# Sums of squares from two rounded parts instead of one float32 product, in a GLA and MLA layer

## The chip, the core and the metric

The kernel runs on one core of one Trainium2 chip. The metric is the device time of one execution in microseconds (us); lower is better. Three runs of the kernel before gave 1149.85, 1149.23 and 1146.63 us, so the median is 1149.23 us.

## What is computed

The reference is two layers over 1024 latent tokens of width 1024. The first layer mixes tokens by gated linear attention (GLA, 4 heads, value width 128) and by multi-head latent attention (MLA); the second by Fourier mixing and spatial gating. Only two places of the first layer matter here, both an RMS normalisation:

```python
def rms_norm(x, g):
    xf = x.astype(jnp.float32)
    y = xf * lax.rsqrt(jnp.mean(xf * xf, -1, keepdims=True) + LN_EPS)
    return (y * g.astype(jnp.float32)).astype(x.dtype)
...
    y_gla = rms_norm(o_gl, gla_norm_g).reshape(B, n, GLA_V_W).astype(h_lat.dtype) * jax.nn.silu(gg_l)
...
    kv = jnp.einsum('bnr,re->bne', rms_norm(ckv, kv_norm_g), w_ukv)...
...
    q = jnp.einsum('bnr,re->bne', rms_norm(cq, q_norm_g), w_uq)...
```

The GLA outputs are normalised per head over 128 channels. The query latents `cq` (rank 256) and the key and value latents `ckv` (rank 128) are normalised over their rank.

## The kernel before, in words

Activations lie transposed, with channels on the 128 partitions and tokens along the free dimension. A sum over channels is therefore a TensorE product with a 128x128 matrix of ones, `k.ones`, which also leaves the sum on every partition.

Most products of the kernel are not plain float32. A tensor is split by `split` (L131) into a rounded part `hi` of type float32r, cast on ScalarE (L136), and a rest `lo`, subtracted on VectorE (L141), and `mm3` (L144) multiplies such parts in three float32r products (L146 to L148). The sums of squares are an exception: they are plain float32 products.

**The GLA outputs** are made by `gla_b` (L673), once for each of four heads, in two halves of 512 tokens. A half is summed in a PSUM bank `po` (L733, L736), squared by ScalarE into `sq` (L741), and after a yield multiplied by the ones (L744). Logarithm and exponential on ScalarE turn the sum into the inverse root, VectorE scales `po` by it (L749), and a transfer that POOL issues puts the result into DRAM (L750). That is 8 sums of 512 columns.

**The latents** are normalised by `rms_T` (L814). It loads one or two blocks (L820), squares them (L824), sums the squares with the ones (L828), refines the inverse root on VectorE (L836 to L839), scales (L843) and stores (L844). `rms_ckv` (L847) calls it for blocks of 512, 512 and 256 tokens with one part; `rms_cq` (L852) for two blocks of 512 with two parts. That is 7 float32 products, 6 of 512 columns and one of 256.

**Order.** The work is written as generators that yield a cost, and `weave` (L51) always advances the stream that is furthest behind its budget. `rms_ckv` runs between the first two heads' `gla_a`, woven with the projection of the GLA values (L486) and with `ada_rest` (L771), which adds up modulation weights on VectorE (L805). `rms_cq` runs beside `gla_b` of the third head. All of `gla` is woven with `in_proj_b` (L531), which projects the input by three-product groups and evacuates each group through a scratch tile `ev` (L189 to L191). The tile framework then fixes the order of each engine's instructions when the program is built, and that is not strictly the order of the source.

**Buffers.** Scratch tiles of 128x512 come from `w2` (L97), a pool of 8 buffers that all streams share. PSUM banks come from a pool of 8. ScalarE table loads for another function are held behind all earlier uses of the old table (`act`, L108).

Of the kernel before, what the change touches and what calls it, by code (L numbers as in the profile page):

```python
# [12 lines left out]
F32 = mybir.dt.float32  # L13
F32R = mybir.dt.float32r
# [6 lines left out]
P = 128  # L21
# [10 lines left out]
def f32(ap):  # L32
    return ap.bitcast(F32)
# [184 lines left out]
def consts(k):  # L218
    nc, A = k.nc, k.A
    c = k.cpool  # L220
    k.ident = c.tile([P, P], F32, name="ident")
    make_identity(nc, k.ident)
    k.eps_c = c.tile([P, 1], F32, name="eps_c")
    nc.vector.memset(k.eps_c, EPS)
    k.one_c = c.tile([P, 2], F32, name="one_c")
    nc.vector.memset(k.one_c, 1.0)
    k.mhalf = c.tile([P, 32], F32, name="mhalf")
    nc.vector.memset(k.mhalf, -0.5)
    k.ones = c.tile([P, P], F32, name="ones")
    nc.vector.memset(k.ones, 1.0)  # L230


def load_norm(k, src):
# [436 lines left out]
    yield 4.0  # L670


def gla_b(k, hd, S):  # L673

    nc = k.nc
    T = nc.tensor
# [23 lines left out]
    for i in range(15):  # L700
        nc.vector.scalar_tensor_tensor(
            out=Tst[(i + 1) // 8][:, (i + 1) % 8, :], in0=Tst[i // 8][:, i % 8, :], scalar=w[:, i:i + 1],
# [9 lines left out]
    for b in range(2):  # L712
# [6 lines left out]
        for c in range(2):  # L719
            r = slice(64 * c, 64 * c + 64)  # L720
            v = [x[r].rearrange("p (t x) -> p t x", x=P)[:, :, r] for x in pa]
# [6 lines left out]
    for b in range(2):  # L728
        att = k.att[:, b]
        po = k.bank("pso")  # L730
        for t in range(4):
            i = 4 * b + t
            T.matmul(po[:, t * P:(t + 1) * P], k.gv[i // 2][:, i % 2, vs], att[:, t, :], start=True, stop=False)  # L733
            for c in range(2):
                ch = 2 * i + c
                T.matmul(po[:, t * P + 64 * c:t * P + 64 * c + 64], Tch[ch // 8][:, ch % 8, :], qh[:, ch * 64:ch * 64 + 64], start=False, stop=c == 1)  # L736
            if t == 1:
                yield 1.3

        sq = k.w2(name="sq")  # L740
        nc.scalar.activation(out=sq, in_=po, func=AF.Square)  # L741
        yield 2.0
        pv = k.bank("psvar")
        T.matmul(pv, k.ones, sq, start=True, stop=True)  # L744
        rs = sq
        k.act(rs, pv, AF.Ln, scale=1.0 / P, bias=k.eps_c)
        k.act(rs, rs, AF.Exp, scale=-0.5)
        og = k.w2(name="og")
        nc.vector.scalar_tensor_tensor(out=og, in0=po, scalar=k.gng, in1=rs, op0=ALU.mult, op1=ALU.mult)  # L749
        nc.gpsimd.dma_start(k.ogd[hd][:, b * 512:(b + 1) * 512], og)  # L750
        yield 2.0
# [5 lines left out]
def gla(k):  # L757
    k.ogd = [k.spill(f"ogd{i}") for i in range(4)]
    k.att = k.b4(F32, (P, 2, 4, P), name="att")
    k.nc.gpsimd.memset(k.att, 0.0)  # L760
    for hd in range(4):
        st = [(gla_b(k, hd, k.S[hd]), 24.0)]
        if hd < 2:
            st.append((gla_a(k, hd + 2, k.S[hd + 2]), 20.0))
        elif hd == 2:
            st.append((rms_cq(k), 12.0))
        yield from weave(*st)
    k.gla_done = True
# [45 lines left out]
def rms_T(k, dr, o, rank):  # L814

    nc = k.nc
    n = o.stop - o.start
    x = [k.w2(name="rmx") for _ in dr]
    for i, d in enumerate(dr):
        nc.sync.dma_start(x[i][:, :n], d[:, o])  # L820
    yield 1.0
    sq = [k.w2(name="rms") for _ in range(2)]
    for i in range(len(dr)):
        nc.scalar.activation(out=sq[i][:, :n], in_=x[i][:, :n], func=AF.Square)  # L824
    yield 1.0
    v = k.bank("psrms")
    for i in range(len(dr)):
        nc.tensor.matmul(v[:, :n], k.ones, sq[i][:, :n], start=i == 0, stop=i == len(dr) - 1)  # L828
    yield 1.0
    y, q = sq[0][:, :n], sq[1][:, :n]  # L830
    t = k.w2(name="rmt")
    k.act(y, v[:, :n], AF.Ln, scale=1.0 / rank, bias=k.eps_c)
    k.act(y, y, AF.Exp, scale=-0.5)

    nc.scalar.activation(out=q, in_=y, func=AF.Square)
    nc.vector.tensor_scalar(out=t[:, :n], in0=v[:, :n], scalar1=1.0 / rank, scalar2=EPS, op0=ALU.mult, op1=ALU.add)  # L836
    nc.vector.tensor_tensor(out=t[:, :n], in0=t[:, :n], in1=q, op=ALU.mult)
    nc.vector.tensor_scalar(out=t[:, :n], in0=t[:, :n], scalar1=-0.5, scalar2=1.5, op0=ALU.mult, op1=ALU.add)
    nc.vector.tensor_tensor(out=y, in0=t[:, :n], in1=y, op=ALU.mult)  # L839
    for i, d in enumerate(dr):  # L840
        xi = x[i][:, :n]
        g = k.mlag[:, i:i + 1] if len(dr) == 2 else k.mlag[:, 2:3]
        nc.vector.scalar_tensor_tensor(out=xi, in0=xi, scalar=g, in1=y, op0=ALU.mult, op1=ALU.mult)  # L843
        nc.gpsimd.dma_start(d[:, o], xi)  # L844


def rms_ckv(k):  # L847
    for s, n in KBLK:
        yield from rms_T(k, [k.ckvd], slice(s, s + n), 128)


def rms_cq(k):  # L852
    assert k.cq_done
    for s in range(0, N, 512):
        yield from rms_T(k, k.cqd, slice(s, s + 512), 256)
        yield 3.0
# [752 lines left out]
```

## Time and profile before

| | us |
|---|---|
| median of 3 runs | 1149.23 |
| the profiled execution | 1150.0 |
| its span, first to last instruction | 1147.5 |
| TensorE matmul (PE) busy in the span | 1091.7 |
| VectorE (DVE) busy | 739.0 |
| ScalarE (ACT) busy | 556.6 |
| GpSimd (POOL) busy | 260.1 |

PE is the matmul side of TensorE and PEld its weight loads, which overlap the matmuls. The mean granted TensorE clock of the span was 0.985 of full speed. Rows of a timeline give the start, the duration and the instruction, with the idle time before it in brackets; the end of a matmul is modelled, so the start of the next one says how long TensorE was taken.

### The profile page before, as it was taken

How to read it: one execution, taken by the hardware profiler on the slowest of the kernel's cores; microseconds unless marked ns; L12 is line 12 of the kernel's file. 1: busy time of each engine (PE TensorE's matmuls, PEld its weight loads, DVE VectorE, ACT ScalarE, POOL GpSimd, SP SyncE). 2: the span in 40 equal slices, each digit the busy share in tenths (PEclk: the TensorE clock that was granted, in tenths of full speed). 3: DMA queues.
4: the chain of work that ended last, by engine and by line, in shares of the span. 5: the costliest groups of instructions: out<-in, count | busy, mean ns of one | idle time of the engine just before them, and what ended most of it. 6: DMA issues, size and time to landing. Idle time of an engine off the chain costs nothing.

```text
span 1147.5 us, 14546 instructions
## 1 busy us (share of the span) xinstructions
PE 1091.7 (95%) x5288; PEld 864.4 (75%) x5288; DVE 739.0 (64%) x1256; ACT 556.6 (49%) x956; POOL 260.1 (23%) x260
## 2 busy tenths in 40 slices
PE   5889999899999999999999999999999999999997
PEld 3668778677777777767677666888788888888885
DVE  6867784756655675765778677788526533664544
ACT  6285755576553367857767778313422223332000
POOL 3520000000000023332424466343101000022111
PEclk8989999899999999999999999999999999999999
DMA  9635662333435752113202424323400311125111
GB/s 373 243 127 194 210 229 101 118 119 111 183 120 178 240 156 52 24 47 88 66 4 51 124 74 137 121 110 134 160 1 1 109 38 56 55 69 200 62 55 55
DMA packets 41752, 131.89 MB, mean 115 GB/s; under 512 B 5673, under 2 KB 7465, under 8 KB 41682
## 3 DMA queue, kind: packets, MB, share of 16 engines
q1 hardware_dynamic: 35578, 114.77, 30.5%
q0 software_dynamic: 3312, 10.26, 2.3%
q10 hardware_dynamic: 2792, 5.94, 1.3%
q8 instruction: 41, 0.67, 0.2%
q14 instruction: 29, 0.24, 0.1%
HBM read 98.37 MB, written 20.36 MB: 103 GB/s over the span
## 4 chain that ended last, share of the span: by engine, by line
PE 75%; DVE 8%; ACT 7%; issue 4%; POOL 3%; DMA 3%; SPq 1%; POOLq 0%; DVEq 0%; ACTq 0%
PE ps L146 10%; PE ps L147 10%; PE ps L148 10%; PE pso L146 5%; PE pso L147 5%; PE pso L148 5%; PE pss L1068 3%; PE psm L993 3%; PE pss L1069 3%; PE pss L1070 3%; PE psav L1054 3%; PE psav L1053 2%; PE psav L1052 2%; PE psn L146 1%; PE psn L147 1%
## 5 line engine op out<-in xcount | busy, mean ns | idle before, releaser
L141 POOL TENSOR_TENSOR ph<-pexp,ph 128x512 fp32r<-128x512 f32 x80 | 108.2, 1357 | 167.8 <-ACT ph L136 145.3
L118 ACT ACTIVATE pexp<-pss 128x512 f32<-128x512 f32 x160 | 93.2, 596 | 61.1 <-PE pss L1070 59.4
L146 PE MATMUL ps<-h,hi 128*128 128x512 f32 x256 | 103.8, 417 | 7.4 <-ACT h L328 3.3
L994 DVE TENSOR_REDUCE mx<-psm 128x1 f32<-128x512 f32 (+1 forms) x192 | 102.5, 592 | 10.7 <-PE psm L993 10.3
L148 PE MATMUL ps<-h,lo 128*128 128x512 f32 x256 | 102.6, 401 | 2.8 <-DVE lo L305 1.5
L147 PE MATMUL ps<-h,hi 128*128 128x512 f32 x256 | 104.2, 407 | 0.8 <-DVE h L329 0.8
L141 DVE TENSOR_TENSOR ph<-pexp,ph 128x512 fp32r<-128x512 f32 x80 | 75.1, 943 | 44.6 <-ACT ph L136 42.9
L141 DVE TENSOR_TENSOR lo<-wraw,hi 128x1024 fp32r<-128x1024 f32 x37 | 47.1, 1283 | 85.0 <-ACT hi L136 80.0
L146 PE MATMUL pso<-hi,yh 128*128 128x512 f32 x256 | 99.8, 390 | 0.0
L147 PE MATMUL pso<-lo,yh 128*128 128x512 f32 x256 | 99.7, 390 | 0.0
L148 PE MATMUL pso<-hi,yl 128*128 128x512 f32 x256 | 99.0, 389 | 0.0
L136 ACT CAST ph<-pexp 128x512 fp32r<-128x512 f32 x160 | 95.2, 620 | 2.8
L146 PE MATMUL ps<-h1h,hi 128*128 128x512 f32 x192 | 75.2, 391 | 0.0
L147 PE MATMUL ps<-h1l,hi 128*128 128x512 f32 x192 | 74.7, 389 | 0.0
L148 PE MATMUL ps<-h1h,lo 128*128 128x512 f32 x192 | 74.7, 389 | 0.0
L1135 POOL TENSOR_TENSOR owr<-owr,rowB 128x1024 f32<-128x1024 f32 x16 | 42.8, 2684 | 119.7 <-DMA owr<-wo 119.6
L1054 PE MATMUL psav<-ph,V 128*96 128x512 f32 x160 | 64.0, 400 | 2.5 <-POOL ph L141 2.2
L146 PEld LDWEIGHTS ps<-h,hi 128*128 128x128 f32 x256 | 49.2, 194 | 20.4 <-ACT h L328 4.8
L1052 PE MATMUL psav<-ph,V 128*96 128x512 f32 x160 | 63.2, 395 | 0.2
L148 PEld LDWEIGHTS ps<-h,lo 128*128 128x128 f32 x256 | 49.1, 192 | 16.7 <-DVE lo L305 2.6
L147 PEld LDWEIGHTS ps<-h,hi 128*128 128x128 f32 x256 | 49.4, 193 | 11.3 <-issue 1.7
L148 PEld LDWEIGHTS pso<-hi,yl 128*128 128x128 f32 x256 | 48.1, 188 | 10.1
(359 smaller groups left out, 2590.9 us busy)
## 6 DMA issues: line engine op xcount, KB each, us to landing
aw<-ada SPq DMA_DIRECT2D x32, 512.0 KB, 7.4
araw<-ada SPq DMA_DIRECT2D x32, 512.0 KB, 4.9
wraw<-we SPq DMA_DIRECT2D x16, 512.0 KB, 6.0
owr<-wo SPq DMA_DIRECT2D x16, 512.0 KB, 4.6
xr<-x SPq DMA_DIRECT2D x16, 512.0 KB, 6.9
wraw<-wd SPq DMA_DIRECT2D x12, 512.0 KB, 3.5
xt<-x SPq DMA_DIRECT2D x8, 512.0 KB, 6.0
kt<-kn SPq DMA_DIRECT2D x16, 256.0 KB, 3.6
```

The costliest lines, as they stand in the source:

```text
L118: r = self.nc.scalar.activation(out=out, in_=in_, func=func, **kw)
L136: self.nc.scalar.copy(out=hi, in_=src)
L141: (lo_eng or self.nc.vector).tensor_tensor(out=lo, in0=src, in1=f32(hi), op=ALU.subtract)
L146: t.matmul(out, lhs[0], rhs[0], start=start, stop=False)
L147: t.matmul(out, lhs[0], rhs[1], start=False, stop=False)
L148: t.matmul(out, lhs[1], rhs[0], start=False, stop=stop)
L993: T.matmul(ps[:, :n], q[0][0:96, i * P:(i + 1) * P], cols(kt[0], s, n)[0:96], start=True, stop=True)
L994: nc.vector.reduce_max(out=mx[:, i, b:b + 1], in_=ps[:, :n], axis=AX.X)
L1052: T.matmul(a[0:96, :], vhi(j, hd), hi, start=j == 0, stop=False)
L1054: T.matmul(a[0:96, :], vhi(j, hd), lo, start=False, stop=j == NK - 1)
L1068: T.matmul(ps, kc[0], q[0][:, o], start=True, stop=False)
L1135: k.nc.gpsimd.tensor_tensor(out=raw, in0=raw, in1=k.ogate, op=ALU.mult)
```

## The change

The ones are made once as a float32r tile, through a scratch tile and a ScalarE copy; `k.ones` becomes a float32 view of that tile. A new function `sums` splits every tile of squares into its rounded part and the rest, in four or two new scratch tiles from `w2`, and multiplies each part by the float32r ones, all accumulated in one bank. It takes the place of the float32 products of `gla_b` and `rms_T`. In `rms_T` all parts are split before the first product.

```diff
-    k.ones = c.tile([P, P], F32, name="ones")
-    nc.vector.memset(k.ones, 1.0)
+    ones = k.w2((P, P), name="ones")
+    nc.vector.memset(ones, 1.0)
+    k.ones_r = c.tile([P, P], F32R, name="ones_r")
+    nc.scalar.copy(out=k.ones_r, in_=ones)
+    k.ones = f32(k.ones_r)
...
+def sums(k, parts):
+
+    split = [k.split(x, None, alloc=lambda dt, shape, name: k.w2(x.shape, dt, name)) for _, x in parts]
+    for i, ((out, _), z) in enumerate(zip(parts, split)):
+        for j in range(2):
+            k.nc.tensor.matmul(out, k.ones_r, z[j], start=i == j == 0, stop=j == 1 and i == len(parts) - 1)
...
         pv = k.bank("psvar")
-        T.matmul(pv, k.ones, sq, start=True, stop=True)
+        sums(k, [(pv, sq)])
...
     v = k.bank("psrms")
-    for i in range(len(dr)):
-        nc.tensor.matmul(v[:, :n], k.ones, sq[i][:, :n], start=i == 0, stop=i == len(dr) - 1)
+    sums(k, [(v[:, :n], z[:, :n]) for z in sq[:len(dr)]])
```

## Rows read from the trace of the kernel before

**Rows 1.** The page: busy shares, and the chain that ended last by engine

```profile
PE 1091.7 (95%) x5288; PEld 864.4 (75%) x5288; DVE 739.0 (64%) x1256; ACT 556.6 (49%) x956; POOL 260.1 (23%) x260
...
PE 75%; DVE 8%; ACT 7%; issue 4%; POOL 3%; DMA 3%; SPq 1%; POOLq 0%; DVEq 0%; ACTq 0%
```

**Rows 2.** Windows: stretch, PE, PEld, DVE, ACT, POOL busy us (count), clock, DMA share, GB/s

```profile
150.00:215.00 65.00, 60.23 (x343) 48.20 (x341) 48.76 (x82) 34.83 (x75) 4.67 (x6) 1.00 0.49 169
215.00:345.00 130.00, 124.39 (x877) 99.47 (x878) 77.12 (x168) 79.02 (x149) 6.47 (x12) 0.96 0.36 124
```

**Rows 3.** The tiles of the two sums: count, min/median/max ns, first and last start

```profile
L744 PEld LDWEIGHTS psvar<-sq,ones x16: 186/188/191, 236.7 to 339.8; 128*128 128x128 f32 x16
L744 PE MATMUL psvar<-sq,ones x16: 591/592/697, 236.7 to 340.2; 128*128 128x512 f32 x16
...
L828 PE MATMUL psrms<-rms,ones x14: 377/592/697, 157.9 to 303.0; 128*128 128x512 f32 x12, 128*128 128x256 f32 x2
```

**Rows 4.** PE timeline: a float32 pair, and float32r matmuls one behind another

```profile
242.45 1.02 PE L744 MATMUL psvar<-sq,ones 128*128 128x512 f32 x2
243.31 0.60 PE L688 MATMUL pskn<-ident,dup 128*128 128x128 f32 x4
...
255.21 0.39 PE L147 MATMUL ps<-h,hi 128*128 128x512 f32 x1
255.44 0.39 PE L148 MATMUL ps<-h,lo 128*128 128x512 f32 x1
```

**Rows 5.** Casts of L136 and subtractions of L141, SBUF to SBUF, by tile

```profile
L136 ACT CAST ghl<-za x8: 606/617/619, 137.7 to 257.8; 128x512 fp32r<-128x512 f32 x8
L136 ACT CAST gc<-za x4: 404/406/409, 128.8 to 248.0; 128x256 fp32r<-128x256 f32 x4
...
L141 DVE TENSOR_TENSOR ghl<-za,ghl x8: 682/692/693, 138.5 to 258.4; 128x512 fp32r<-128x512 f32 x8
L141 DVE TENSOR_TENSOR gc<-za,gc x4: 418/422/426, 129.2 to 248.4; 128x256 fp32r<-128x256 f32 x4
```

**Rows 6.** Timeline of ACT around the first half of the second head

```profile
273.47 0.29 ACT L682 COPY Tst<-sctx 128x128 f32<-128x128 f32 x1
...
275.37 0.60 ACT L741 ACTIVATE sq<-pso 128x512 f32<-128x512 f32 x1
```

**Rows 7.** What PE waited for from 130 to 350 us: total us, times, longest

```profile
PE pskc L619 <- DVE ec L615: 6.8, 3, 3.6
PE psrms L828 <- ACT rms L824: 2.1, 3, 1.2
PE pso L733 <- DVE att L724: 0.8, 2, 0.5
```

**Rows 8.** Timeline of ACT at the start and at the end of GLA

```profile
2.19 1.06 ACT L118 ACTIVATE crow<-crow 1x1024 f32<-1x1024 f32 x1 [0.18 <-DMA crow<-c]
...
342.25 1.28 ACT L114 ACT_TABLE_LOAD   x1
```

**Rows 9.** PE timeline and clock around the longest wait inside GLA

```profile
212.45 0.39 PE L148 MATMUL ps<-h,lo 128*128 128x512 f32 x1
216.42 0.66 PE L619 MATMUL pskc<-ident,ec 128*128 128x128 f32 x2 [3.58 <-DVE ec L615]
216.73 0.78 PE L146 MATMUL ps<-h,hi 128*128 128x512 f32 x1
217.30 0.63 PE L147 MATMUL ps<-h,hi 128*128 128x512 f32 x1
...
215.00:220.00 5.00, 3.58 (x12) 2.58 (x14) 2.69 (x6) 3.35 (x8) 0.00 (x0) 0.52 0.14 52
220.00:225.00 5.00, 5.00 (x42) 4.25 (x42) 1.74 (x4) 0.27 (x1) 0.00 (x0) 0.79 0.00 0
```

**Rows 10.** A wait of ACT inside `rms_cq`, and the transfer's time to landing

```profile
299.95 0.63 ACT L824 ACTIVATE rms<-rmx 128x512 f32<-128x512 f32 x1 [4.24 <-DMA mgd<-ev]
...
mgd<-ev ACTq DMA_DIRECT2D x8, 256.0 KB, 3.4
```

## The prediction

> **What bounds the kernel now.** I read the page first. TensorE's matmul side is busy for 95% of the span, VectorE for 64%, ScalarE for 49%, and three quarters of the chain that ended last is TensorE [rows 1]. So TensorE time that is saved is worth something, as long as the other engines don't make TensorE stand in its place. Then I cut the span by windows, since all of the change lies between 150 and 345 us [rows 2, 3]. The `ckv` sums fall into the first 65 us of it, where VectorE is the most loaded of the helpers (48.8 of 65 us). The eight GLA sums and the two `cq` blocks fall into the next 130 us, where PE is busy for 124.4, VectorE for 77.1 and ScalarE for 79.0 [rows 2]. The tiles of the sums give their counts and durations, the timeline of TensorE what they really hold it for, and the list of waits what TensorE stands for today. A difference of less than 0.3% of the time, 3.4 us, could not be told from no change here.
>
> **What is removed.** A float32 product is a pair of matmul instructions [rows 3]. Their durations overlap, so I take starts: the pair begins at 242.45 and the next matmul at 243.31, so it holds TensorE for 0.86 us [rows 4]. Two float32r matmuls of the same width start 0.23 us apart [rows 4], so the new pair holds it for 0.46 us. The saving is 0.40 us for each of 8 GLA sums and 6 latent products of 512 columns, 5.6 us. For the one of 256 columns I take half, 0.2 us, as an estimate. In all 5.8 us.
>
> A rule speaks against this term. The Trainium skill, page "Perfetto Trace Analysis", section "Identifying the Most-Contended Engine", judges TensorE's headroom by the busy time of its weight loads and not by that of its matmuls. By it the term would be zero, for the float32 pair has two loads and the new pair has two.
>
> The rows decide otherwise: the two loads take 0.38 us [rows 3], less than half of the 0.86 us that the pair holds the engine, so there it is the streaming that is cut. The new pair, at 0.46 us, still lies above its loads. I keep 5.8 us.
>
> **What is added on ScalarE and VectorE.** There are 15 casts and 15 subtractions. The nearest rows are the same operations from scratch to scratch: a cast of 512 columns takes 0.62 us, of 256 columns 0.41; a subtraction 0.69 and 0.42 [rows 5]. That is 14 x 0.62 + 0.41 = 9.1 us on ScalarE and 14 x 0.69 + 0.42 = 10.1 us on VectorE. Of it, 12 casts (7.4 us) and 12 subtractions (8.3 us) fall into the 130 us window, which brings ScalarE to 86.4 and VectorE to 85.4 of 130 us, both two thirds. Three of each fall into the first window, where VectorE goes from 48.8 to 50.6 of 65 us [rows 2]. I cost this work as such at nothing: the projections on TensorE cover it. If that cover went, it would be the 1.31 us chain below.
>
> **What is added as a wait.** The product used to need the squares alone; now it needs a cast and a subtraction behind them, 0.62 + 0.69 = 1.31 us more [rows 5], and 2.0 us for a `cq` block, where two subtractions follow one another. There are 13 such points, 8 of GLA, 3 of `ckv`, 2 of `cq`. Behind the cast on ScalarE stand evacuations and exponentials, behind the subtraction on VectorE the scaling of other outputs and the modulation sums; behind the product on TensorE stand the woven projection groups. The low end is nothing: the GLA sum has no entry among TensorE's waits today [rows 7], and the engines' orders are made at build time with later work let past. The third head's first copy, L682, runs ahead of the second head's square, which stands before it in the source [rows 6]. So projection matmuls can be put in front of a sum that is not ready. The high end is that TensorE stands for the whole new chain each time, 11 x 1.31 + 2 x 2.0 = 18.4 us. In between lie two rows of products that take a result just made by another engine: the GLA product waits 0.8 us over 8 halves for the mask on VectorE, 0.10 each, and the latent sums wait 2.1 us over 5 blocks, 0.42 each [rows 7]. These are the rows nearest to the new case, and both lie near the low end. I take 0.10 for each GLA half, and for each latent block half as much again as it waits today, 0.2: 0.8 + 1.0 = 1.8 us.
>
> **Small edits.** The copy of the ones stands on ScalarE at about 2 us, between the table load and the first SiLU, which begins at 2.19 when its transfer lands [rows 8]. A copy of 128x128 takes 0.29 us [rows 6], so the SiLU may be late by 0 to 0.3 us; it heads the start chain, and I take 0.1. Every later float32 use of the ones reads the same values and costs the same. The last two GLA halves have a second follower: the ScalarE table load at 342.25 [rows 8] comes behind the last exponential and moves 1.3 us later with it. What it feeds, the gating of projected tiles, is scheduled after it in any case and TensorE has projection groups left, so nothing is charged; the end for this is 0 to 1.3 us.
>
> **Sum.** 5.8 saved, less 1.8 of new waits, less 0.1 at the start: 3.8 us. In the profiled execution's own time that is 1150.0 - 3.8 = 1146.2 us. That execution is 0.8 us above the median of the three runs, so against 1149.2 I expect **1145.4 us**.
>
> **Rivals.**
>
> *The saving is stood away (no change).* TensorE takes matmuls strictly in the order of the program: at 216.42 it had waited 3.58 us for a transpose's operand while the second half of a projection group, begun before, stood ready behind it [rows 9]. If a sum is placed one projection step too early, TensorE stands for 1.31 us; 4 or 5 of the 13 points doing so eat 5.8 us, and the time is 1149 us. Eight of them would make 1154. For it: these waits exist for other products [rows 7], and the subtraction adds a second engine whose backlog must be foreseen. Against it: the present sum never waits.
>
> The Trainium skill states the same order, in "TensorE: Matmul & The Clock Gate", section "Part 3: Packing small matmuls — row/col tiling": matmuls start and end strictly in sequence. The trace agrees with it, by the 3.58 us.
>
> *The scratch pool runs dry (slower).* A `cq` block holds two loaded tiles and two squares, and now four parts before its first product: eight, all that the pool has, while evacuations and GLA halves use the same pool. Today ScalarE already waits 4.24 us inside the second block for an evacuated tile's transfer, whose landing takes 3.4 us [rows 10]. If each of the two blocks sends one such wait through to TensorE, it stands 4.2 us, and after a wait of that length it runs slow: after the 3.58 us the granted clock is 0.52 and then 0.79 in two stretches of five us, near the lower of its two levels of 1.2 and 2.4 GHz at first, and two matmuls start 0.57 us apart [rows 9]. That clock costs 5 x 0.48 + 5 x 0.21 = 3.5 us. Two blocks give 2 x 7.7 = 15.4, less the 5.7 us saved: 1159 us. It decides against the change once more than some 9 us of standing reach TensorE (5.7 + 3.4). Against it: projection groups have banks of their own, and the orders are made with the pool known.
>
> *A present wait goes (much faster).* The change shifts VectorE's and ScalarE's order from 157 us on. If the 3.58 us wait [rows 9] and the slow clock after it vanish, 7.1 us come on top: 1138 us. Nothing in the change aims at it, but that wait hangs on the order of VectorE.
>
> *The change does not do what it says:* the float32r pair runs no faster than the float32 pair, 1149 to 1151 us. The rate of float32r here is that of all projections [rows 4], so this is very unlikely.
>
> **How the numbers follow.** The forecast gets 0.52; its own range is 1142 to 1148.5, from waits of 0 to 4 us, and it splits into 0.34 beyond the bound and 0.18 within, since 1145.4 lies just past 3.4 us. The stood-away saving gets 0.22, 0.18 within and 0.04 slower. The dry pool gets 0.12, slower. The vanished wait gets 0.12, faster. No effect of the type gets 0.02, within. Faster: 0.34 + 0.12 = 0.46. Same: 0.18 + 0.18 + 0.02 = 0.38. Slower: 0.04 + 0.12 = 0.16. The range is 1139 to 1153: it leaves out the dry pool (0.12), a little below (0.05) and the worst of the stood-away case (0.03).
>
> **What would show it.** Right: the tiles of both sums show matmuls starting 0.23 us apart; PE busy falls by about 6 us; casts and subtractions of 0.62 and 0.69 us appear for the squares; TensorE's waits for these subtractions add up to less than 3 us. Wrong: one line of these waits above 5 us, ScalarE or VectorE waiting for transfers of evacuated tiles between 285 and 315 us, a second stretch of low clock there, or a wait at 212 us that is gone or doubled, which would mean that the new order weighs more than the products themselves.

## The result and the profile after

| | before | after |
|---|---|---|
| median, us (6 runs each) | 1149.05 | 1160.22 |
| lowest to highest, us | 1145.66 to 1149.85 | 1154.74 to 1165.17 |
| the profiled execution, us | 1150.0 | 1154.74 |
| its span, us | 1147.5 | 1153.0 |

The changed kernel is slower: the ratio is 1.0102, with an interval of 1.0064 to 1.0139, or 11.7 us (7.4 to 16.0) on 1149. The forecast was 3.8 us faster; the time lies outside the range, on its upper side.

The profiled execution of the changed kernel is the fastest of its six. The other five, from 1155.67 to 1165.17 us, have mean granted clocks between 0.972 and 0.985, the profiled one 0.983, and there is no trace of them. The trace therefore shows a loss of 5.5 us of span, half of the measured one; the ratios of the experiments below stand for whole sets of runs.

The page's busy times [rows 1]:

```profile
PE 1088.1 (94%) x5288; PEld 863.7 (75%) x5288; DVE 748.6 (65%) x1271; ACT 566.4 (49%) x972; POOL 261.1 (23%) x260
```

VectorE has 9.6 us more and ScalarE 9.8, which is the work that was counted (10.1 and 9.1). TensorE is busy for 3.6 us less, and yet the span is longer: the loss is time in which TensorE stands. The two windows of the prediction say where [rows 2]:

```profile
150.00:215.00 65.00, 56.70 (x310) 45.92 (x309) 43.35 (x73) 29.93 (x66) 3.57 (x5) 0.92 0.46 162
215.00:345.00 130.00, 116.31 (x875) 94.49 (x874) 89.20 (x190) 87.52 (x164) 6.35 (x11) 1.00 0.32 111
```

Between 150 and 215 us TensorE does 33 matmuls fewer than before in the same time, and the granted clock is 0.92 where it was 1.00. In the second window it is busy for 8.1 us less, of which 12 x 0.40 = 4.8 are the saving of the 12 products there. The low clock that stood near 217 us before [rows 9] is gone in this trace, which shortens the busy time too: the second window has 1.00 where it had 0.96.

The list of TensorE's waits from 130 to 350 us (total, times, longest) names them [rows 7]. `psrms` are the sums of the latents, `psvar` those of GLA, `pskc` is a transpose in `gla_a`:

```profile
PE psrms L681 <- ACT hi L136: 5.9, 4, 3.3
PE psrms L681 <- DVE lo L141: 5.5, 3, 3.1
PE pskc L622 <- DVE ec L618: 5.0, 3, 3.5
PE psvar L681 <- ACT hi L136: 2.9, 3, 1.4
```

The latents' sums waited 2.1 us for their squares. Now they wait 11.4 us for the casts and the subtractions, and the GLA sums, which had no entry, 2.9 us. That is 12.2 us more, over twice the 5.8 us that the products save. The 5.5 us of span that this execution lost are close to the difference, 6.4 us.

Most of it is in one place. The products of `ckv` in the kernel before, and the group in front of them (start, duration, instruction, idle time before it and its releaser):

```profile
156.20 1.88 PE L791 MATMUL ps<-acc,ones 128*128 128x512 f32 x4
157.91 1.02 PE L828 MATMUL psrms<-rms,ones 128*128 128x512 f32 x2
...
162.89 1.12 PE L828 MATMUL psrms<-rms,ones 128*128 128x512 f32 x2 [1.21 <-ACT rms L824]
...
168.21 0.59 PE L828 MATMUL psrms<-rms,ones 128*128 128x256 f32 x2
```

And the first two blocks in the changed kernel:

```profile
156.57 1.88 PE L802 MATMUL ps<-acc,ones_r 128*128 128x512 f32 x4
...
160.14 0.39 PE L681 MATMUL psrms<-hi,ones_r 128*128 128x512 f32 x1
160.37 0.39 PE L148 MATMUL ps<-hi,h 128*128 128x512 f32 x1
...
161.05 0.39 PE L148 MATMUL ps<-hi,h 128*128 128x512 f32 x1
162.37 0.50 PE L681 MATMUL psrms<-lo,ones_r 128*128 128x512 f32 x1 [0.94 <-DVE lo L141]
166.14 0.79 PE L681 MATMUL psrms<-hi,ones_r 128*128 128x512 f32 x1 [3.27 <-ACT hi L136]
166.73 0.63 PE L146 MATMUL ps<-hi,h 128*128 128x512 f32 x1
170.41 0.79 PE L681 MATMUL psrms<-lo,ones_r 128*128 128x512 f32 x1 [3.05 <-DVE lo L141]
171.00 0.63 PE L147 MATMUL ps<-lo,h 128*128 128x512 f32 x1
171.43 0.63 PE L148 MATMUL ps<-hi,h 128*128 128x512 f32 x1
```

The product with the rounded part of block 2 stands directly behind the product with the rest of block 1, with nothing between them, and the rest of block 2 comes one projection matmul later. TensorE has three waits, 7.3 us in all, and does three matmuls between the first and the last of them. Behind the last one stand projection matmuls that start one behind the other as soon as it is done.

In the kernel before, 12 projection matmuls stood between the sums of blocks 1 and 2 and 19 between those of 2 and 3, and the one wait among them was 1.2 us. Counted from the same group (L791 before, L802 after), the first products of blocks 2 and 3 have not moved: 12 and 31 projection matmuls stand ahead of them in either kernel. Block 1's have. The program that was built put 8 projection matmuls in front of its first product and 12 in front of its second, where none stood before, and so used up the gap ahead of block 2.

The Trainium skill, "TensorE: Matmul & The Clock Gate", section "Part 3: Packing small matmuls — row/col tiling", has matmuls start and end strictly in sequence. The trace agrees, by the same 3.05 us in which no later projection matmul went ahead.

ScalarE's timeline says why the second cast came so late:

```profile
159.23 0.62 ACT L136 CAST hi<-rms 128x512 fp32r<-128x512 f32 x1
...
162.91 0.69 ACT L118 ACTIVATE rms<-psrms,eps_c 128x512 f32<-128x512 f32 x1 [0.85 <-PE psrms L681]
163.62 0.63 ACT L118 ACTIVATE rms<-rms 128x512 f32<-128x512 f32 x1
164.28 0.63 ACT L845 ACTIVATE rms<-rms 128x512 f32<-128x512 f32 x1
164.82 0.61 ACT L835 ACTIVATE rms<-rmx 128x512 f32<-128x512 f32 x1
165.47 0.62 ACT L136 CAST hi<-rms 128x512 fp32r<-128x512 f32 x1
```

And VectorE's, why both subtractions did:

```profile
157.80 3.92 DVE L816 SCALAR_TENSOR_TENSOR acc<-araw,small,acc 128x1024 f32<-128x1024 f32 x3
161.63 0.68 DVE L141 TENSOR_TENSOR lo<-rms,hi 128x512 fp32r<-128x512 f32 x1
...
167.81 1.28 DVE L816 SCALAR_TENSOR_TENSOR acc<-araw,small,acc 128x1024 f32<-128x1024 f32 x1
169.01 0.75 DVE L853 SCALAR_TENSOR_TENSOR rmx<-rmx,small,rms 128x512 f32<-128x512 f32 x1
169.67 0.68 DVE L141 TENSOR_TENSOR lo<-rms,hi 128x512 fp32r<-128x512 f32 x1
```

Read as one chain: the first cast is done by 159.9, but its subtraction queues behind three modulation sums until 161.63. Only then comes block 1's second product, at 162.37, and only then its root on ScalarE: logarithm, exponential and square. Block 2's square and cast stand behind that root, so that its first product comes at 166.14. Block 2's subtraction stands behind the end of block 1's root and two modulation sums on VectorE, until 169.67. Two blocks that used to overlap run one after the other through three engines, and TensorE stands in each turn.

Afterwards TensorE is slow. Windows of the changed kernel, with the clock in the third column from the end:

```profile
150.00:160.00 10.00, 10.00 (x42) 7.61 (x41) 9.13 (x17) 3.69 (x9) 0.00 (x0) 1.00 0.58 216
160.00:170.00 10.00, 3.15 (x10) 1.54 (x8) 7.99 (x11) 3.67 (x6) 0.00 (x0) 0.73 0.66 237
170.00:180.00 10.00, 9.59 (x37) 7.87 (x38) 7.18 (x11) 4.80 (x11) 1.12 (x2) 0.76 0.34 118
```

TensorE is busy for 3.15 of the ten microseconds from 160, and the granted clock falls from 1.00 to 0.73 and 0.76. Between 171.00 and 171.43 two projection matmuls start 0.43 us apart, near the lower of the two levels (1.2 of 2.4 GHz), where they start 0.23 apart before (160.14 to 160.37). As an estimate, at 0.76 the second ten microseconds cost 10 x 0.24 = 2.4 us on top of the waits. In the same two stretches of the kernel before the clock was 1.00.

The second block of `cq` shows the other new wait. ScalarE and VectorE:

```profile
312.30 0.62 ACT L136 CAST hi<-rms 128x512 fp32r<-128x512 f32 x1 [4.26 <-DMA cqd<-rmx]
```
```profile
311.11 0.69 DVE L141 TENSOR_TENSOR lo<-rms,hi 128x512 fp32r<-128x512 f32 x1 [1.45 <-DMA cqd<-rmx]
```

Both wait for the first block's store, `cqd<-rmx`, since the new parts need the scratch buffers that it still holds. TensorE waits 1.88, 1.46 and 0.23 us in that block, and 0.48 us in the first, 4.1 us in all.

How far the loss reaches: the first sum of a GLA half starts at 242.7 us instead of 236.7, the first attention score (`pss`) at 423.6 instead of 417.0, the first product of the output projection (`pso` from `yh`) at 713.9 instead of 708.4, which is already the 5.5 us of the span. In this trace nothing more is lost after the first attention score.

### The profile page after: what moved, and what is told of

Its sections match the earlier page's. It is cut to its first block, busy times and chain, and to the rows that moved or that the text cites. A ratio compares the mean times of both kernels' runs of the same rounds, so it can differ in the third digit from the quotient of the medians.

```text
span 1153.0 us, 14571 instructions
## 1 busy us (share of the span) xinstructions
PE 1088.1 (94%) x5288; PEld 863.7 (75%) x5288; DVE 748.6 (65%) x1271; ACT 566.4 (49%) x972; POOL 261.1 (23%) x260
## 4 chain that ended last, share of the span: by engine, by line
PE 74%; issue 8%; DVE 7%; ACT 6%; POOL 3%; DMA 2%; SPq 0%; POOLq 0%; DVEq 0%; ACTq 0%
PE ps L146 10%; PE ps L147 10%; PE ps L148 10%; PE pso L148 5%; PE pso L146 5%; PE pso L147 5%; PE psm L1003 3%; PE pss L1078 3%; PE pss L1079 3%; PE pss L1080 3%; PE psav L1064 3%; PE psav L1063 2%; PE psav L1062 2%; PE psn L146 1%; PE psn L148 1%
## 5 line engine op out<-in xcount | busy, mean ns | idle before, releaser
L141 POOL TENSOR_TENSOR ph<-pexp,ph 128x512 fp32r<-128x512 f32 x80 | 108.1, 1355 | 166.5 <-ACT ph L136 139.2
L146 PE MATMUL ps<-h,hi 128*128 128x512 f32 x256 | 102.3, 411 | 8.2 <-ACT h L331 3.3
L141 DVE TENSOR_TENSOR ph<-pexp,ph 128x512 fp32r<-128x512 f32 x80 | 75.0, 943 | 45.8 <-ACT ph L136 42.7
L147 PE MATMUL ps<-h,hi 128*128 128x512 f32 x256 | 101.6, 397 | 0.8 <-DVE h L332 0.8
L136 ACT CAST ph<-pexp 128x512 fp32r<-128x512 f32 x160 | 95.3, 620 | 2.8
L141 DVE TENSOR_TENSOR lo<-wraw,hi 128x1024 fp32r<-128x1024 f32 x37 | 44.9, 1224 | 76.4 <-ACT hi L136 71.4
L148 PEld LDWEIGHTS pso<-hi,yl 128*128 128x128 f32 x256 | 48.1, 188 | 10.1
```

The source lines that it names most:

```text
L136: self.nc.scalar.copy(out=hi, in_=src)
L141: (lo_eng or self.nc.vector).tensor_tensor(out=lo, in0=src, in1=f32(hi), op=ALU.subtract)
L146: t.matmul(out, lhs[0], rhs[0], start=start, stop=False)
L147: t.matmul(out, lhs[0], rhs[1], start=False, stop=False)
L148: t.matmul(out, lhs[1], rhs[0], start=False, stop=stop)
```

## The experiments

Each kernel ran in five rounds beside the kernel before, whose medians in the four batches were 1149.39, 1148.94, 1149.96 and 1148.99 us. The ratios are those on record; they differ a little from the quotients of the medians. "Waits in `ckv`" are TensorE's for the parts or squares from 150 to 190 us; "all" adds `cq` and the GLA sums; both are from one trace each.

| kernel | waits in `ckv`, us | all, us | median, us | ratio to before (interval) |
|---|---|---|---|---|
| before | 1.2 | 2.1 | 1149.05 | |
| after | 7.3 | 14.3 | 1160.22 | 1.0102 (1.0064 to 1.0139) |
| e1 GLA halves only | 1.2 | 7.2 | 1153.15 | 1.0027 (1.0014 to 1.0040) |
| e2 latents only | 7.2 | 10.3 | 1159.21 | 1.0085 (1.0060 to 1.0109) |
| e8 ckv only | 7.3 | 8.5 | 1158.10 | 1.0066 (1.0046 to 1.0086) |
| e9 cq only | 1.2 | 4.1 | 1152.29 | 1.0023 (1.0005 to 1.0041) |
| e4 all splits early | 3.6 | 6.0 | 1150.30 | 1.0003 (0.9982 to 1.0023) |
| e15 ckv early, rest as after | 3.6 | 8.8 | 1154.84 | 1.0049 (1.0029 to 1.0069) |
| e13 ckv blocks spaced | 4.2 | 9.6 | 1154.12 | 1.0040 (1.0019 to 1.0061) |
| e11 products a step later | 8.5 | 14.5 | 1160.12 | 1.0096 (1.0077 to 1.0115) |
| e14 early, ckv products later | 4.0 | 6.3 | 1151.39 | 1.0025 (1.0008 to 1.0042) |
| e10 GLA only, early | 1.2 | 3.6 | 1148.18 | 0.9991 (0.9973 to 1.0009) |
| e12 early, ckv float32 | 1.2 | 3.6 | 1146.93 | 0.9974 (0.9960 to 0.9988) |
| e7 rounded squares only | 2.8 | 3.6 | 1144.49 | 0.9949 (0.9929 to 0.9969) |
| e3 parts in the big pool | 3.8 | 7.7 | 1161.09 | 1.0092 (1.0070 to 1.0115) |
| e5 after, 10 scratch buffers | 8.0 | 15.2 | 1168.14 | 1.0149 (1.0126 to 1.0172) |
| e6 before, 10 scratch buffers | 1.2 | 1.2 | 1148.14 | 0.9991 (0.9977 to 1.0004) |

### Which sums lose: the halves and the latents apart

e1 puts the latents' sums back:

```diff
-    sums(k, [(v[:, :n], z[:, :n]) for z in sq[:len(dr)]])
+    for i in range(len(dr)):
+        nc.tensor.matmul(v[:, :n], k.ones, sq[i][:, :n], start=i == 0, stop=i == len(dr) - 1)
```

> Only the eight GLA sums are made from two parts; the latents' sums are float32 products again. Theory of the scratch pool (the loss comes from the latents' blocks, whose new parts don't fit into 8 scratch buffers): 1145 to 1149 us, TensorE waits for psrms as before (about 2 us) and for psvar under 4 us. Rival of the helpers' load (every split makes TensorE stand, GLA as much as latents): about half of the loss stays, 1152 to 1156 us.

e2 puts the GLA sums back:

```diff
-        sums(k, [(pv, sq)])
+        T.matmul(pv, k.ones, sq, start=True, stop=True)
```

> Only the latents' sums are made from two parts; the GLA sums are float32 products again. Scratch pool: the whole loss, 1155 to 1165 us, with TensorE waiting over 8 us for psrms and a second stretch of low clock between 160 and 180 us. Helpers' load: about half of the loss, 1152 to 1156 us, with waits for psrms of about 5 us.

e1 took 1153.15 us, 0.27% over the kernel before: the halves alone lose too, where 3.2 us (8 x 0.40) were to be saved. e2 took 1159.21, 0.85% over. So about three quarters of the two together are in the latents. TensorE's first waits in e2 are those of the changed kernel (0.94, 3.34 and 2.98 us). Neither theory holds for both: e1's time lies in the range of the helpers' load, e2's in that of the scratch pool.

### Is it the number of scratch buffers

The scratch pool of `w2` gets two buffers more, for one of the 48 large ones, in the changed kernel (e5) and in the kernel before (e6):

```diff
-    k.wk, k.big = enter(pool("work", 8)), enter(pool("big", 48))
+    k.wk, k.big = enter(pool("work", 10)), enter(pool("big", 47))
```

> The changed kernel with 10 scratch buffers in place of 8, paid for with one of the 48 big buffers. Scratch pool: waits of TensorE for psrms fall from 11.4 to under 4 us, ScalarE no longer waits for the store of the first cq block, and the time comes to 1143 to 1149 us. Helpers' load: no change, 1154 to 1165 us.

> Control: the kernel before with 10 scratch and 47 big buffers. Both theories: within 4 us of the kernel before, 1145 to 1153 us; the scratch pool's theory adds that ScalarE's wait of 4.24 us for an evacuated tile's transfer goes.

The theory of a dry pool as the main cause fell: with ten buffers the changed kernel took 1168.14 us, slower still, and its waits in `ckv` stayed, 3.27 us for block 2's rounded part and 3.14 us for its rest. Nor did TensorE's waits in `cq` fall, 4.1 us as in the changed kernel: ScalarE no longer waits for the store of the first block, but VectorE still does, 1.99 us, ahead of the last subtraction. The control shows that ten buffers by themselves change nothing that can be told (0.9991). Why e5 is worse still was not settled; its list has a wait of 3.8 us for the cast `gc` in front of L608 that the changed kernel doesn't have.

### ckv or cq

In e8 only a block with one part goes through `sums`, in e9 only a block with two; the GLA sums are float32 products in both, as in e2.

```diff
-    sums(k, [(v[:, :n], z[:, :n]) for z in sq[:len(dr)]])
+    if len(dr) == 1:
+        sums(k, [(v[:, :n], z[:, :n]) for z in sq[:len(dr)]])
+    else:
+        for i in range(len(dr)):
+            nc.tensor.matmul(v[:, :n], k.ones, sq[i][:, :n], start=i == 0, stop=i == len(dr) - 1)
```

> Only the three blocks of ckv are summed from two parts; cq and the GLA halves are summed as float32 products. Theory A (nearly all the loss is made in the ckv blocks): TensorE's waits for hi and lo in 150 to 172 us stay near 8 us, the first sum of a GLA half comes at 241 us or later, and the time is 1154 to 1161 us. Rival D (cq block 2, whose scratch buffers run dry, makes about half of what the latents lose): the time is 1150 to 1154 us.

> Only the two blocks of cq are summed from two parts, split and products where the change has them; ckv and the GLA halves are float32 products. Theory A (the cq blocks make the smaller part of the loss, the scratch buffers of block 2 running dry): ScalarE waits 3 to 5 us in block 2 as in the changed kernel, TensorE 3 to 4 us, and the time is 1149 to 1153 us. Rival H (the recorded price of dry scratch buffers, the wait in both blocks and a slow clock behind each): 1157 us or more.

The three sums of `ckv` alone cost 0.66%, 7.6 us; they would have saved 1.0 us. Their waits in e8, from the list between 130 and 350 us:

```profile
PE psrms L681 <- DVE lo L141: 3.7, 2, 2.8
PE psrms L681 <- ACT hi L136: 3.6, 1, 3.6
```

`cq` alone costs 0.23%. ScalarE waits 3.2 us for the store of the first block, as theory A has it, and TensorE stands for 2.9 us in the two blocks. The times of e8 and e9 lie where their theory A had them, and both rivals fell. The parts add: 0.66 + 0.23 = 0.89% beside 0.85% for the latents together, and with the halves 1.16% beside 1.02% for the change, well inside the intervals.

### Emit the split a step earlier

The cast and the subtraction are issued right behind the square, ahead of the yield; the products stay where `sums` has them.

```diff
+    sp = [parts_of(k, z[:, :n]) for z in sq[:len(dr)]]
     yield 1.0
     v = k.bank("psrms")
-    sums(k, [(v[:, :n], z[:, :n]) for z in sq[:len(dr)]])
+    sums(k, [(v[:, :n], z) for z in sp])
```

(the same behind the square of a GLA half; `parts_of` is the `split` that `sums` made)

> The kernel after the change, but the cast and the subtraction are emitted right behind the Square of the block, one step of the interleaving earlier; the products stay where the kernel before had its own, so that projection matmuls stand again in TensorE's program between the products of two blocks of ckv. Theory A (the loss is the order: the products of two blocks stand side by side, and TensorE stands while ScalarE and VectorE bring the second split): TensorE's waits for hi and lo in 150 to 172 us fall from 8.2 us to below 3, its busy time in 150:200 goes from 41.7 us back to 45 to 48, the first sum of a GLA half stands at 236 to 239 us again, and the time is 1146 to 1153 us. Rival B (the cast and the subtraction are paid wherever they are emitted, because ScalarE and VectorE are late with the work that stands in front of the products): the waits stay over 6 us and the time is 1156 to 1162 us.

1150.30 us, ratio 1.0003 (0.9982 to 1.0023): no loss is left that can be told. TensorE's timeline, its sums in `ckv`:

```profile
158.57 0.80 PE L686 MATMUL psrms<-hi,ones_r 128*128 128x512 f32 x1
159.21 0.40 PE L686 MATMUL psrms<-lo,ones_r 128*128 128x512 f32 x1
164.21 0.51 PE L686 MATMUL psrms<-hi,ones_r 128*128 128x512 f32 x1 [1.85 <-ACT hi L136]
166.43 0.50 PE L686 MATMUL psrms<-lo,ones_r 128*128 128x512 f32 x1 [1.72 <-DVE lo L141]
```

The subtraction of block 1 now stands ahead of the three modulation sums on VectorE, so that both its products are done by 159.6. The order of the kernel before is back: none of the projection stands in front of block 1's pair, 12 matmuls between blocks 1 and 2, and 19 between 2 and 3. The waits are 3.6 us where theory A asked for less than 3; they are halved, not gone. (The 8.2 us from which the expectations of this stage start are 4.0 + 3.3 = 7.3 us in the list.) TensorE is busy for 45.3 us from 150 to 200 us, and the first sum of a GLA half stands at 239.0 us, both as theory A had it.

e15 does the same for `ckv` alone, inside the whole change:

> The kernel after the change, with the split of the ckv blocks alone emitted early; cq and the GLA halves as the change has them. Theory A (the parts add: 0.66 % for ckv, 0.27 % for the GLA halves, 0.23 % for cq, each with its late split): ckv's share falls to 0.1 to 0.3 %, and the time is 1153 to 1157 us. Rival I (the parts do not add; one bad place in the latents is enough for the whole loss): 1158 us or more, with cq and the GLA halves taking what ckv gives back.

1154.84 us: `ckv` gives back 0.53 of the 1.02%, near the 0.66% that it costs by itself; the 0.49% that are left agree with what the halves (0.27%) and `cq` (0.23%) cost with their late splits.

### The place of the products, or the lateness of the split

e13 leaves the split where the change has it and puts one step behind each block:

```diff
         yield from rms_T(k, [k.ckvd], slice(s, s + n), 128)
+        yield 2.0
```

> The kernel after the change with one more step of the interleaving behind each block of ckv: split and products are emitted together as the change has them, but in TensorE's program 24 other products stand between the pair of block 1 and that of block 2, and 17 between the pairs of block 2 and block 3. Theory A (pairs side by side make the loss): the waits for hi and lo in ckv fall from 8.2 us to below 4 us and the time is 1149 to 1155 us. Rival B (the lateness of the split makes it, side by side or not): the waits stay at 5 us or more, or what follows comes as late as in the changed kernel, and the time is 1156 to 1162 us.

e11 leaves the split too and moves the products one step behind it:

```diff
     yield 1.0
+    sp = [parts_of(k, z[:, :n]) for z in sq[:len(dr)]]
+    yield 1.0
     v = k.bank("psrms")
```

> The kernel after the change, with the split emitted where the change has it, but the products of the latents one step of the interleaving behind the split (the GLA halves as the change has them). In TensorE's program 24 other products then stand between the pair of ckv block 1 and that of block 2, where the change has none; block 3's pair stands right behind block 2's. Theory A (the order of the products makes the loss): the waits for hi and lo of block 2 fall from 6.3 us to below 2 us, and the time is 1147 to 1154 us, unless block 3's pair now stands for its split instead. Rival B (the late split is the loss, wherever the products stand, since what follows the sums comes later): the time is 1155 to 1162 us.

e14 is e4 with the products of `ckv` another step later:

```diff
     sp = [parts_of(k, z[:, :n]) for z in sq[:len(dr)]]
     yield 1.0
+    if len(dr) == 1:
+        yield 1.0
```

> As the run with all splits emitted early, but in ckv the products come one more step behind their split; the pair of block 2 moves 16 products back in TensorE's program and stands close to that of block 3, and what follows in the same stream comes one step later. Theory A, with the addition that a split emitted a step earlier needs no gap in TensorE's program: the 3.6 us of waits for block 2 fall below 1.5 us and the time is 1145 to 1150 us. Rival B (what counts is how late the whole chain of the blocks ends): the time is 2 to 8 us above that of the run with early splits, 1152 to 1159 us.

Three ways of placing the pairs. In e11, between blocks 1 and 2 stand 24 other products now, and block 3's pair stands right behind block 2's:

```profile
170.59 0.50 PE L686 MATMUL psrms<-hi,ones_r 128*128 128x512 f32 x1 [1.85 <-ACT hi L136]
172.04 0.51 PE L686 MATMUL psrms<-lo,ones_r 128*128 128x512 f32 x1 [0.94 <-DVE lo L141]
175.38 0.58 PE L686 MATMUL psrms<-hi,ones_r 128*128 128x256 f32 x1 [2.84 <-ACT hi L136]
178.33 0.58 PE L686 MATMUL psrms<-lo,ones_r 128*128 128x256 f32 x1 [1.93 <-DVE lo L141]
```

Block 2's waits fell from 6.3 to 2.8 us, which is more than the 2 us expected, and block 3, which didn't wait in the changed kernel, now waits 4.8. The long wait went to whichever block stands close behind the one before it; the time did not move (1160.12), as the rival had it and as theory A's exception for block 3 allowed. e13, which parts all three pairs with the split still late, comes to 1154.12 us, 0.40%, inside theory A's range, and its waits to 4.2 us instead of 7.3, just above the 4 us of theory A. And in e14 the same happens with early splits: block 2's pair, moved back to stand close to block 3's, waits for nothing (164.53 and 165.22), and block 3's, five matmuls behind it, waits 4.1 us:

```profile
168.81 0.39 PE L686 MATMUL psrms<-hi,ones_r 128*128 128x256 f32 x1 [2.04 <-ACT hi L136]
171.69 0.58 PE L686 MATMUL psrms<-lo,ones_r 128*128 128x256 f32 x1 [2.04 <-DVE lo L141]
```

So an early split does not make the gap needless: by the waits my addition that it does fell. In time e14 lies between the ranges of theory and rival, at 1151.39 us, and its interval overlaps that of e4. A pair close behind another waits 4 to 6 us for its split, early or late (after, e11, e14); a pair with its gap waits 1.4 to 3.6 us (e13, e11's block 2, e4).

What stands for the place of the pairs is e13: with the split as late as in the change, spacing takes the loss from 1.02% to 0.40%, nearly all that `ckv` costs by itself. With an early split instead (e15) it is 0.49%, which can't be told from 0.40%. So no cost of the lateness by itself is seen in `ckv`, but the pair is no clean test of it. The added step moves all that follows: TensorE's waits for `pskc` are 0.5 us in e13 and 4.9 in e15.

### The halves and cq with early splits, and without a split

e10 is e1 with the early split; e12 adds `cq` with the early split and leaves `ckv` as float32 products:

> Only the GLA halves are summed from two parts, with the cast and the subtraction emitted right behind the Square; the latents are summed as float32 products as before. Theory A (the two-part sum saves its 0.4 us per sum wherever the split is ready when the products' turn comes): psvar waits fall from the 4.0 us of the run with the GLA halves alone to 2 us or less, the stretch from the first to the last sum of a GLA half shortens from 103.5 us to 99 to 101 us, and the time is 1144 to 1148 us, below the kernel before. Rival F (the saving in the halves stands away in what follows): 1148.5 to 1153 us.

> As the run with the early GLA halves, and the two blocks of cq too are summed from two parts with the early split; only the three blocks of ckv stay float32 products. Theory A (an early split is paid by cover, and cq saves another 4 x 0.4 us): 1143 to 1148 us, at or below the run with the GLA halves alone. Rival G (cq block 2's split waits for scratch buffers also when it is emitted early, and that eats it): ScalarE waits 2 us or more for the store of the first block, and the time is 1 to 4 us above that run.

With the early split the halves no longer lose: 0.9991 against 1.0027. The timelines of e1 and e10 show it in the first half, whose two products were 4.9 us apart behind a late subtraction and are 1.4 us apart behind an early one:

```profile
236.87 0.50 PE L681 MATMUL psvar<-hi,ones_r 128*128 128x512 f32 x1 [0.28 <-ACT hi L136]
241.74 0.39 PE L681 MATMUL psvar<-lo,ones_r 128*128 128x512 f32 x1
```
```profile
236.35 0.50 PE L686 MATMUL psvar<-hi,ones_r 128*128 128x512 f32 x1 [0.27 <-ACT hi L136]
237.72 0.47 PE L686 MATMUL psvar<-lo,ones_r 128*128 128x512 f32 x1
```

From the first sum of a GLA half to the last it takes 102.3 us in e10 (236.4 to 338.7), 107.0 in e1 and 103.5 before; 99 to 101 were expected. Its median, 1148.18 us, lies just past the range of theory A and short of that of rival F, and its interval, 3.1 us faster to 1.0 us slower, holds nearly all of the expected 3.2 us as well as nothing.

e12 takes 1146.93 us, 0.26% under the kernel before, and its interval leaves no change out. No engine waits for the first block's store any more. ScalarE does wait for a scratch buffer in block 2, 2.64 us, but for the subtraction of block 2's first part to give it free, and 0.44 us of waiting for that block reach TensorE. So rival G's wait is there in another form, and costs nothing that shows. e12 is the one version with both parts in its sums that beats both kernels, the kernel before by 3.0 us against the 12 x 0.40 = 4.8 us that its products save. That is under the 0.3% that the prediction took for the least that can be told; the 12 runs of e12 beside 29 of the kernel before give a narrower interval, 0.12% to 0.40%. Its page has as many weight loads as the kernel before:

```profile
PE 1089.2 (95%) x5288; PEld 864.5 (76%) x5288; DVE 745.8 (65%) x1268; ACT 564.0 (49%) x969; POOL 261.2 (23%) x260
```

That bears on the rule that the prediction weighed, of the Trainium skill, "Perfetto Trace Analysis", section "Identifying the Most-Contended Engine", which goes by the busy time of TensorE's weight loads, beside the share of peak arithmetic that the kernel reaches, which the prediction left out. By the loads alone these 12 sums would have saved nothing, since they take 864.5 us where they took 864.4; the time fell by 0.26%.

e7 squares into the rounded type and multiplies once, in the halves and in the latents; it leaves out the rest of each square:

```diff
-        nc.scalar.activation(out=sq[i][:, :n], in_=x[i][:, :n], func=AF.Square)
+        nc.scalar.activation(out=sr[i][:, :n], in_=x[i][:, :n], func=AF.Square)
...
+        nc.tensor.matmul(v[:, :n], k.ones_r, sr[i][:, :n], start=i == 0, stop=i == len(dr) - 1)
```

> The Square writes the rounded type itself, and each sum of squares takes one rounded product: no cast, no subtraction, no second part; what the rounding takes off each square is left out of the sums. Theory A (the rounded type itself saves what the prediction counted, 14 float32 products at 0.86 us against 0.23 us, and the loss is made by the split): TensorE's waits for the squares in the latents stay at the 2 us of before, its busy time falls by 8 to 9 us, and the time is 1138 to 1146 us. Rival E (the saving stands away in TensorE's waits for what follows, so that a cheaper sum is worth nothing here): 1147 to 1151 us.

1144.49 us, 0.51% under the kernel before. A cheaper sum is worth something here, and it is the sum with a split that loses it. TensorE's busy time fell by 5.7 us (to 1086.0) where 8 to 9 were expected, and its waits for the squares are 3.6 us where 2 were; the time fell by 5.9 us.

### Parts in the other pool

e3 keeps both parts of a split in one tile of the pool of large buffers:

```diff
+        z = k.b4(F32R, (P, 2, 512), name="sqp")[:, :, :x.shape[1]]
+        split.append(k.split(x, None, hi=z[:, 0, :], lo=z[:, 1, :]))
```

> The kernel after the change, but both parts of a split lie in one tile of the pool of 2 KB-and-over buffers instead of two scratch tiles. Theory A (the order of the products in ckv; the scratch pool costs the rest, in cq block 2): the 4.26 us that ScalarE and the 1.45 us that VectorE wait in cq block 2 go away; where the new place also parts the products of the first two ckv blocks, the waits for hi and lo in 150 to 172 us fall below 4 us and the time is 1147 to 1154 us. Rival C (the pool is not what holds the splits, but the engines are): ckv keeps 6 us or more of these waits and the time is 1156 to 1162 us.

The waits in `ckv` fell to 3.8 us, as theory A had it for a place that parts the pairs, and ScalarE's wait for the store in `cq` is gone. TensorE waits 0.8 us in `cq` instead of 4.1, which bears out that the scratch buffers held the parts back there. Yet the time is 1161.09 us. In its trace, 11.4 us of span longer than the kernel before, the first sum of a GLA half comes 4.6 us later than before and the last 4.8. At the first attention score it is 9.7 us. Between them lies a stretch from 360 to 380 us where the changed kernel's TensorE is busy for 17.86 us at a clock of 1.00. Here it waits 2.86 and 1.61 us for two parts that a projection needs, and the clock falls:

```profile
360.00:380.00 20.00, 15.53 (x56) 11.97 (x55) 14.75 (x20) 7.26 (x10) 0.54 (x1) 0.83 0.56 184
```

Whether the parts hold buffers that this projection wanted was not tried by itself, and the rest of e3's loss is open.

## Why the prediction was wrong

**The saving was right in size.** A float32r product held TensorE for 0.23 us (160.14 to 160.37), so the pair is 0.46, as worked out. e12 and e7 turn such savings into time. The added work, 9.8 and 9.6 us where 9.1 and 10.1 were counted, was right too, and as work it cost nothing that shows: e12 has 12 of the 15 casts and subtractions and is faster than the kernel before. (The sum 5.8 - 1.8 - 0.1 is 3.9 us and not 3.8; nothing hangs on it.)

**The term that failed is "what is added as a wait".** It was taken at 1.8 us, between 0 and 18.4. TensorE's new waits come to 12.2 us in the trace, inside the bounds but far from the value, and both reasons for the value were wrong:

- The rows taken as nearest, 0.10 and 0.42 us per product, were waits of products in the old order, the latents' with 12 and 19 projection matmuls between their blocks. The term held that order fixed, and the change moved it. That later work can be put in front of a sum was read from two ScalarE instructions [rows 6] and carried over to TensorE. There it held for block 1 of `ckv`, which got 12 projection matmuls in front of its second product. It did not hold for block 2, whose place stayed as it was and which was left with nothing between it and block 1.
- The high end per point, 1.31 us, was the duration of a cast and a subtraction with both engines free. The waits of block 2 were 3.27 and 3.05 us, since each stood in a queue: the cast behind the root of block 1, which itself came late because block 1's subtraction stood behind three modulation sums of 1.28 us; block 2's subtraction behind the end of that root and two more. The sentence that "its backlog must be foreseen" stood in a rival, with no price. The sum of the bounds held only because the GLA halves waited for so little.

**What the waits do not hold.** New waits less saving give 12.2 - 5.8 = 6.4 us for the execution that was profiled, which lost 5.5 us of span: there the waits are the whole of the loss. The median lost 11.7, 5.3 more than this balance. The balance of the trace also falls short of the medians by 4.2 us for e2, 4.4 for e11, 4.5 for e14 and 2.2 for e8 (6.4 - 1.0 = 5.4, where 7.6 were measured), and by 0.3 for e12 (1.5 - 4.8 = -3.3, where -3.0 were).

The record has a number that goes with most of this, the mean granted clock of every execution. It averages 0.983 to 0.984 over the runs of the kernel before in each of the four batches, and 0.983 over those of e12. Over the runs of the change, e2, e8, e11 and e14, in all of which two pairs of `ckv` stand close, it is 0.978 to 0.979; where they have gaps (e4, e13, e15) it is 0.981 to 0.982. As an estimate, 0.983 less 0.9785 is worth 0.0045 x 1149 = 5.2 us. So a lower clock goes with the close pairs and is of the size that is missing for the change. It is not the whole: for e9 2.2 us are missing too (0.4 by the balance, 2.6 measured), at the clock of the kernel before. What lowers it is not shown: the low clock after the 7.3 us of waits is 2.4 us in the one trace, and the executions of the change with the longest times have no trace.

**The rivals.** "The saving is stood away" had the mechanism, TensorE standing in order for a sum placed too early, but at 1.31 us a point it reached only 1154 us, and slower by it had a chance of 0.04. "The scratch pool runs dry" was seen, in `cq` block 2 alone: ScalarE waits 4.26 us for the store, not for an evacuated tile, but TensorE stands 3.6 us there and no low clock follows. By itself that part costs 0.23% (e9), so the rival's 1159 us agree with the result by chance. "A present wait goes" came half true: `pskc` still waits 3.46 us, now at 224.27, but the low clock behind it is gone in this trace. That the type has no effect is refuted by e7.

**The signs named beforehand** did serve: one line of waits above 5 us is there (5.9 and 5.5), and PE busy fell by 3.6 instead of 6 us.

## What to carry to other kernels

When one product becomes two that need a cast and a subtraction, the cost is where the new instructions land in the engines' queues: emit the split right behind what it splits, a step of other work ahead of the product, and look whether the pairs of neighbouring blocks still have work between them. Price a new wait by the queue in front of its producer at that moment (here two or three modulation sums of 1.28 us, and the last block's root), not by the producer's own duration. A loss in one short stage can be found by giving each stage the change alone: three of fifteen sums held more than half of it, and leaving these out and emitting the other splits early made the change a gain.

## What was not expected of the hardware

After a stretch in which TensorE was busy for 3.15 of 10 us, the granted clock was still 0.76 in the next ten, though TensorE was busy for 9.59 of them: matmuls started 0.43 us apart from 171.0 on and 0.23 apart again from 174.8. In this trace a stand of 7 us thus cost about a third more than itself (2.4 of 7.3 us, an estimate).

A stand of half that length went without it. The kernel before had a wait of 3.58 us and then a clock of 0.52 and 0.79 [rows 9]. The changed kernel has the same wait, 3.46 us long and 8 us later, in a stretch where TensorE is busy for 6.54 of ten microseconds, and the clock stays at 1.00:

```profile
220.00:230.00 10.00, 6.54 (x48) 4.91 (x48) 7.13 (x16) 5.86 (x13) 0.00 (x0) 1.00 0.07 26
```

In e8's trace the same wait, 3.43 us up to 224.90, is followed by a low clock again, though TensorE is busy without a break:

```profile
225.00:230.00 5.00, 5.00 (x30) 3.95 (x31) 2.12 (x5) 2.02 (x4) 0.00 (x0) 0.66 0.14 52
```

No run here shows what sets these apart, so a price of the clock per wait, as the dry-pool rival had it, is not safe.

Two more scratch buffers left the kernel before where it was (0.9991), and the changed kernel, with 1.0149 beside 1.0102, no better and probably worse.
